# The last row tile of a matmul with layer norm: three quarters normalised from PSUM by VectorE, one quarter by GpSimd, stores on two queues

## The chip, the cores and the metric

The kernel runs on one core of a Trainium2 chip. The metric is the device time of one execution in microseconds, a median over runs. All times in this text are microseconds unless marked ns. One execution was recorded by the hardware profiler; its instruction times count from the start of its span, which runs from the first to the last recorded instruction. Differences of up to about 0.2% (0.5 us) can't be told from no change in this kernel.

## The reference

The inputs are `a` and `b`, both 2048 x 2048 in fp32, two vectors `gamma` and `beta` of length 2048, and a scalar `eps`.

```
x = np.matmul(a, b)
mean = np.mean(x, axis=-1, keepdims=True)
var = np.var(x, axis=-1, keepdims=True)
normalized = (x - mean) / np.sqrt(var + eps)
return (gamma * normalized + beta).astype(np.float32)
```

Each row of the product needs its mean and variance over all 2048 columns before any element of that row can be written out.

## The kernel before

The 2048 rows are cut into 16 row tiles of 128 rows (one row per partition), and each row tile into four quarters of 512 columns, numbered q = 0 to 3. A quarter is one PSUM bank: 128 x 512 fp32, written by 16 matmuls over the 16 blocks of the inner dimension (`mm`, line 99, fp16 operands). `b` stays in SBUF as fp16. Row tiles of `a` are transposed by TensorE or by DMA ahead of their use.

The first four row tiles are computed together while `a` and `b` arrive. From row tile 4 on the main loop (line 304) takes one row tile after the other, quarter by quarter. After a quarter's 16 matmuls, `evacuate` (lines 104 to 110) has ScalarE copy the bank into the SBUF tile `x` (line 109), and VectorE then reads that copy for the quarter's statistics (`bn_stats`, line 110). When the fourth quarter is in, `stats` (line 114) merges the four sets of statistics into mean and variance (`bn_aggr`, line 116), adds `eps` (line 118), and ScalarE takes the square root (line 120). VectorE's `reciprocal` (`inv`, line 141) gives `rstd`.

The normalisation of a quarter is two VectorE instructions in place on the SBUF tile, each a `scalar_tensor_tensor` over 128 x 512 fp32: `centre` (line 125), (x - mean) * gamma, and `scale` (line 131), x * rstd + beta. `store` (line 137) then issues a DMA to the output from the SP queue.

The schedule is written by hand: every engine executes its instructions in the order of the program. For all row tiles but the last, the normalisation is queued as two pieces in `backlog` and issued between the evacuations of the next row tile, so that VectorE does it while TensorE computes. For the last row tile (i = 15, lines 323 to 335) there is no next one. Nothing but its own normalisation and its four stores of 256 KB follows the last matmul: centre 0 and 1, rstd, scale and store 0, scale and store 1, centre 2 and 3, scale and store 2, scale and store 3. At the very end every engine waits until the SP engine has seen all DMA semaphores (line 366, the launch).

DMA semaphores go round: eight are used in turn by the DMAs that SP issues. The last four stores have the seventh, the eighth, the first and the second of them.

Of the kernel before, what the change touches and what calls it, by code (L numbers as in the profile page):

```python
# [9 lines left out]
FP32 = mybir.dt.float32  # L10
FP16 = mybir.dt.float16
AluOp = mybir.AluOpType
# [4 lines left out]
def kernel(  # L17
# [9 lines left out]
    nc = tc.nc  # L27
    P = 128
    M, K = a.shape
    K2, N = b.shape  # L30
# [3 lines left out]
    NB = 512  # L34
    n_nb = N // NB
# [18 lines left out]
    xpool = ctx.enter_context(tc.tile_pool(name="xpool", bufs=7))  # L54
    stat = ctx.enter_context(tc.tile_pool(name="stat", bufs=6))
# [8 lines left out]
    gamma_b = konst.tile([P, N], FP32)  # L64
    beta_b = konst.tile([P, N], FP32)
# [4 lines left out]
    xs = [None] * n_mt  # L70
    bnst = [None] * n_mt
    acc = {}
# [16 lines left out]
    def transpose_blocks(i, k0, n):  # L89

        t_ps = psum.tile([P, n, P], FP16, tag="ps", name=f"tps{i}_{k0}")
        for j in range(n):
            nc.tensor.transpose(t_ps[:, j, :], a16[i][:, ts(k0 + j, P)], ident)  # L93
        nc.scalar.copy(at[i][:, ds(k0, n), :], t_ps)  # L94

    def mm(i, q, kt):
        if (i, q) not in acc:
            acc[i, q] = bank(f"acc{i}_{q}")
        nc.tensor.matmul(  # L99
            acc[i, q], at[i][:, kt, :], b16[:, kt, ds(q * NB, NB)],  # L100
            start=(kt == 0), stop=(kt == n_kt - 1),
        )

    def evacuate(i, q):
        if xs[i] is None:
            xs[i] = xpool.tile([P, N], FP32, tag="x", name=f"x{i}")
            bnst[i] = stat.tile([P, n_nb, 6], FP32, tag="bnst", name=f"bnst{i}")
        qs = ds(q * NB, NB)
        nc.scalar.copy(xs[i][:, qs], acc[i, q])  # L109
        nc.vector.bn_stats(bnst[i][:, q, :], xs[i][:, qs])  # L110

    backlog = []

    def stats(i):
        mv = stat.tile([P, 2], FP32, tag="mv", name=f"mv{i}")
        nc.vector.bn_aggr(mv, bnst[i])  # L116
        ve = stat.tile([P, 1], FP32, tag="ve", name=f"ve{i}")
        nc.vector.tensor_tensor(ve, mv[:, 1:2], eps_t, AluOp.add)  # L118
        sq = stat.tile([P, 1], FP32, tag="sq", name=f"sq{i}")
        nc.scalar.activation(sq, ve, ActFn.Sqrt)  # L120
        return mv, sq

    def centre(i, q, mv):
        qs = ds(q * NB, NB)
        nc.vector.scalar_tensor_tensor(  # L125
            xs[i][:, qs], xs[i][:, qs], mv[:, 0:1], gamma_b[:, qs],
            AluOp.subtract, AluOp.mult)

    def scale(i, q, rstd):
        qs = ds(q * NB, NB)  # L130
        nc.vector.scalar_tensor_tensor(  # L131
            xs[i][:, qs], xs[i][:, qs], rstd, beta_b[:, qs],
            AluOp.mult, AluOp.add)

    def store(i, q0, nq):
        s = ds(q0 * NB, nq * NB)
        nc.sync.dma_start(out[ts(i, P), s], xs[i][:, s])

    def inv(i, sq):
        rstd = stat.tile([P, 1], FP32, tag="rstd", name=f"rstd{i}")  # L140
        nc.vector.reciprocal(rstd, sq)  # L141
        return rstd

    def queue_norm(i, mv, sq):

        got = {}

        def piece(q0):
            def run():
                centre(i, q0, mv)  # L150
                centre(i, q0 + 1, mv)
                if q0 == 0:
                    got["rstd"] = inv(i, sq)
                scale(i, q0, got["rstd"])
                scale(i, q0 + 1, got["rstd"])
                store(i, q0, 2)
            return run

        backlog.extend(piece(q) for q in range(0, n_nb, 2))

    def drain(n):
        for _ in range(min(n, len(backlog))):
            backlog.pop(0)()


    nc.vector.memset(zeros, 0.0)  # L166
    nc.vector.memset(ident, 0.0)
    nc.gpsimd.affine_select(
        out=ident, in_=ident, compare_op=AluOp.not_equal, fill=1.0,
# [92 lines left out]
    for what in order:  # L262
        if what[0] == "a":
            _, i, c = what
# [19 lines left out]
    for q in (2, 3):  # L284
# [3 lines left out]
        for p in range(n_open):  # L288
# [3 lines left out]
            if q == 3:  # L292
                mv, sq = stats(p)
# [10 lines left out]
    for i in range(n_open, n_mt):  # L304
        last = i == n_mt - 1
        if i + 1 < n_pe:
            at[i + 1] = atp.tile([P, n_kt, P], FP16, tag="at", name=f"at{i + 1}")
        if n_pe <= i + 3 < n_mt:
            at[i + 3] = atp.tile([P, n_kt, P], FP16, tag="at", name=f"at{i + 3}")
            nc.sync.dma_start_transpose(at[i + 3][:, :, :], a16[i + 3])  # L310
        for q in range(n_nb):
            for kt in range(n_kt):
                mm(i, q, kt)
                if i + 1 < n_pe and kt == 8 and q in (1, 2):
                    transpose_blocks(i + 1, (q - 1) * (n_kt // 2), n_kt // 2)
            evacuate(i, q)
            if q < n_nb - 1:
                drain(1)
        mv, sq = stats(i)
        if not last:  # L320
            queue_norm(i, mv, sq)
            drain(1)
        else:
            drain(len(backlog))
            for q in (0, 1):
                centre(i, q, mv)
            rstd = inv(i, sq)
            for q in (0, 1):
                scale(i, q, rstd)
                store(i, q, 1)  # L330
            for q in (2, 3):
                centre(i, q, mv)
            for q in (2, 3):
                scale(i, q, rstd)
                store(i, q, 1)


# [1 line left out]
_INS = ['a', 'b', 'gamma', 'beta', 'eps']  # L339
_OUTS = [((2048, 2048), 'float32')]  # L340
# [30 lines left out]
```

## Time and profile before

| what | us |
|---|---|
| median of 3 runs | 255.78 (255.48 to 255.9) |
| the profiled execution, its device time | 255.81 |
| its span | 254.0 |
| device time beyond the span | 1.8 |
| PE busy | 238.3 (94%) |
| DVE busy | 154.0 (61%) |
| ACT busy | 60.2 (24%) |
| POOL busy | 26.0 (10%) |

PE is TensorE, DVE is VectorE, ACT is ScalarE, POOL is GpSimd and SP is the engine that issues most DMAs; a name with a q behind it (SPq) is that engine's instruction queue. A group line gives line of the code, engine, operation, output and input tile with shapes and count, then busy time and the mean duration of one, then idle time of the engine before them and what ended it. A timeline line gives start, duration, engine, line and operation. A row may merge several instructions (x2).

TensorE is busy almost throughout, and its granted clock was 0.986 of full speed over the span. The last matmuls end at about 242.8, and 11 us of the span follow.

### The profile page before, as it was taken

How to read it: one execution, taken by the hardware profiler on the slowest of the kernel's cores; microseconds unless marked ns; L12 is line 12 of the kernel's file. 1: busy time of each engine (PE TensorE's matmuls, PEld its weight loads, DVE VectorE, ACT ScalarE, POOL GpSimd, SP SyncE). 2: the span in 40 equal slices, each digit the busy share in tenths (PEclk: the TensorE clock that was granted, in tenths of full speed). 3: DMA queues.
4: the chain of work that ended last, by engine and by line, in shares of the span. 5: the costliest groups of instructions: out<-in, count | busy, mean ns of one | idle time of the engine just before them, and what ended most of it. 6: DMA issues, size and time to landing. Idle time of an engine off the chain costs nothing.

```text
span 254.0 us, 3029 instructions
## 1 busy us (share of the span) xinstructions
PE 238.3 (94%) x1182; PEld 110.4 (43%) x1182; DVE 154.0 (61%) x275; ACT 60.2 (24%) x106; POOL 26.0 (10%) x52
## 2 busy tenths in 40 slices
PE   8899989999989999999999999999999999999920
PEld 3345444444444444454444444444444444444400
DVE  1555556203037999998959284765648291938563
ACT  2133216112074225232112121212121121112110
POOL 0000047767100001001000000000000000000000
PEclk9999999999999999999999999999999999999995
DMA  5999969999999759998996617090806222220304
GB/s 171 385 399 400 400 240 137 181 153 181 335 253 215 167 206 235 203 270 232 228 319 167 157 50 197 1 247 3 225 23 157 93 83 83 83 85 33 132 2 163
DMA packets 32782, 46.33 MB, mean 182 GB/s; under 512 B 18432, under 2 KB 22528, under 8 KB 32512
## 3 DMA queue, kind: packets, MB, share of 16 engines
q1 hardware_dynamic: 26144, 33.56, 39.9%
q0 software_dynamic: 6624, 12.59, 27.3%
q8 instruction: 9, 0.15, 0.2%
q14 instruction: 5, 0.04, 0.0%
HBM read 35.65 MB, written 16.78 MB: 206 GB/s over the span
## 4 chain that ended last, share of the span: by engine, by line
PE 80%; DMA 12%; DVE 3%; ACT 2%; SPq 0%; issue 0%; DVEq 0%
PE acc L99 79%; DMA b_st<-in_b_dram 7%; DMA a_st<-in_a_dram 5%; PE tps L93 1%; DVE x L125 1%; ACT at L94 1%; DVE x L131 1%; ACT x L109 1%; DVE bnst L110 1%; ACT L120 1%; DVE b L204 0%; DVEq L366 0%; DVE mv L116 0%; SPq L188 0%; ACT sq L120 0%
## 5 line engine op out<-in xcount | busy, mean ns | idle before, releaser
L99 PE MATMUL acc<-b,at 128*128 128x512 f16 x1024 | 225.3, 379 | 3.2 <-DVE b L204 1.5
L99 PEld LDWEIGHTS <-at 128*128 128x128 f16 x1024 | 99.2, 98 | 121.1 <-issue 3.3
L110 DVE BATCH_NORM_STATS2 bnst<-x 128x6 f32<-128x512 f32 x64 | 44.2, 691 | 74.0 <-ACT x L109 73.9
L109 ACT COPY x<-acc 128x512 f32<-128x512 f32 x64 | 37.5, 586 | 130.7 <-PE acc L99 130.5
L131 DVE SCALAR_TENSOR_TENSOR x<-x,rstd,beta_b 128x512 f32<-128x512 f32 x64 | 45.1, 746 | 0.6
L125 DVE SCALAR_TENSOR_TENSOR x<-x,mv,gamma_b 128x512 f32<-128x512 f32 x64 | 44.9, 743 | 0.0
L94 ACT COPY at<-tps 128x512 f16<-128x512 f16 (+1 forms) x24 | 17.4, 727 | 33.2 <-PE tps L93 33.2
L204 DVE CAST b<-b_st 128x1024 f16<-128x1024 f32 x16 | 11.1, 694 | 14.2 <-DMA b_st<-in_b_dram 14.2
L83 POOL DMA_DIRECT2D b<-in_b_dram x32 | 17.5, 551 | 6.4 <-DMA b<-in_b_dram 4.3
L303 POOL DMA_DIRECT2D a<-in_a_dram x11 | 5.8, 531 | 64.1 <-DMA at<-a 44.0
L93 PEld LDWEIGHTS <-a 128*128 128x128 f16 x128 | 9.2, 98 | 6.0 <-issue 0.6
L93 PE MATMUL tps<-ident,a 128*128 128x128 f16 x128 | 11.1, 219 | 0.1
L231 PE MATMUL warm<-zeros 128*128 128x512 f16 x30 | 9.2, 441 | 1.2 <-DVE zeros L166 1.2
L201 DVE CAST a<-a_st 128x512 f16<-128x512 f32 x16 | 6.8, 427 | 5.3 <-DMA a_st<-in_a_dram 5.3
L120 ACT ACTIVATE sq<-ve 128x1 f32<-128x1 f32 x16 | 3.2, 203 | 20.1 <-DVE ve L118 20.1
L231 PEld LDWEIGHTS <-zeros 128*128 128x128 f16 x30 | 3.1, 111 | 4.7 <-issue 2.1
L116 DVE BATCH_NORM_AGGREGATE mv<-bnst 128x2 f32<-128x24 f32 x16 | 4.2, 264 | 0.6
L212 POOL COPY gate<-b_st 128x1 f32<-128x1 f32 x1 | 0.7, 707 | 33.6 <-DMA b_st<-in_b_dram 33.6
L118 DVE TENSOR_TENSOR ve<-mv,eps_t 128x1 f32<-128x1 f32 x16 | 2.5, 159 | 0.5
L141 DVE RECIPROCAL rstd<-sq 128x1 f32<-128x1 f32 x16 | 2.5, 156 | 0.0
L94 ACT ACT_TABLE_LOAD x1 | 1.3, 1283 | 0.7 <-PEq L352 0.7
L120 ACT ACT_TABLE_LOAD x1 | 1.3, 1283 | 0.0
(11 smaller groups left out, 2.7 us busy)
## 6 DMA issues: line engine op xcount, KB each, us to landing
out_dram<-x SPq DMA_DIRECT2D x30, 512.0 KB, 3.5
b_st<-in_b_dram SPq DMA_DIRECT2D x16, 512.0 KB, 7.8
a<-in_a_dram POOLq DMA_DIRECT2D x12, 512.0 KB, 9.1
a_st<-in_a_dram SPq DMA_DIRECT2D x16, 256.0 KB, 7.2
b<-in_b_dram POOLq DMA_DIRECT2D x32, 128.0 KB, 5.7
gamma_b<-in_gamma_dram POOLq DMA_DIRECT2D x1, 1024.0 KB, 9.9
beta_b<-in_beta_dram POOLq DMA_DIRECT2D x1, 1024.0 KB, 12.8
out_dram<-x SPq DMA_DIRECT2D x4, 256.0 KB, 2.6
```

Source lines behind the costliest of these rows:

```text
L83: nc.gpsimd.dma_start(b16[:, kt, ds(c0, w)], b[ts(kt, P), ds(c0, w)])
L93: nc.tensor.transpose(t_ps[:, j, :], a16[i][:, ts(k0 + j, P)], ident)
L94: nc.scalar.copy(at[i][:, ds(k0, n), :], t_ps)
L99: nc.tensor.matmul(acc[i, q], at[i][:, kt, :], b16[:, kt, ds(q * NB, NB)], start=(kt == 0), stop=(kt == n_kt - 1),)
L109: nc.scalar.copy(xs[i][:, qs], acc[i, q])
L110: nc.vector.bn_stats(bnst[i][:, q, :], xs[i][:, qs])
L120: nc.scalar.activation(sq, ve, ActFn.Sqrt)
L125: nc.vector.scalar_tensor_tensor(xs[i][:, qs], xs[i][:, qs], mv[:, 0:1], gamma_b[:, qs], AluOp.subtract, AluOp.mult)
L131: nc.vector.scalar_tensor_tensor(xs[i][:, qs], xs[i][:, qs], rstd, beta_b[:, qs], AluOp.mult, AluOp.add)
L201: nc.vector.tensor_copy(a16[i][:, ts(c, KW)], a_st[c][:, ts(i, KW)])
L204: nc.vector.tensor_copy(b16[:, k, 0:NH], b_st[k // 2][:, ts(k % 2, NH)])
L231: nc.tensor.matmul(warm, zeros[:, 0:P], zeros, start=True, stop=True)
```

## The change

For row tile 15 `evacuate` is replaced by `evacuate_last`: only quarter 1 is still copied to SBUF by ScalarE; the statistics of all four quarters are read by VectorE straight from the PSUM banks. The tail is replaced by `finish`: quarters 0, 2 and 3 are normalised by VectorE, the first step in place in PSUM (`first`) and the second from PSUM into the SBUF tile (`second`); quarter 3's second step is cut into two halves of 256 columns, each with a store of its own. Quarter 1 is normalised by GpSimd in three instructions from the SBUF copy. Quarters 2 and 1 are stored from the SP queue, quarter 0 and the halves of quarter 3 from the ACT queue. VectorE's new order is first 2, first 3, rstd, first 0, second 2, second 0, second 3a, second 3b. Nothing before row tile 15 changes.

```diff
+    PQ = 1
+    def evacuate_last(i, q):
+        if xs[i] is None:
+            xs[i] = xpool.tile([P, N], FP32, tag="x", name=f"x{i}")
+            bnst[i] = stat.tile([P, n_nb, 6], FP32, tag="bnst", name=f"bnst{i}")
+        if q == PQ:
+            nc.scalar.copy(xs[i][:, ds(q * NB, NB)], acc[i, q])
+        nc.vector.bn_stats(bnst[i][:, q, :], acc[i, q])
+
+    def finish(i, mv, sq):
+        x = xs[i]
+        def first(q):
+            nc.vector.scalar_tensor_tensor(
+                acc[i, q], acc[i, q], mv[:, 0:1], gamma_b[:, ds(q * NB, NB)],
+                AluOp.subtract, AluOp.mult)
+        def second(q, c0, w, eng):
+            s = ds(q * NB + c0, w)
+            nc.vector.scalar_tensor_tensor(
+                x[:, s], acc[i, q][:, ds(c0, w)], rstd, beta_b[:, s],
+                AluOp.mult, AluOp.add)
+            eng.dma_start(out[ts(i, P), s], x[:, s])
+        first(2)
+        first(3)
+        rstd = inv(i, sq)
+        s = ds(PQ * NB, NB)
+        nc.gpsimd.tensor_scalar(
+            x[:, s], x[:, s], mv[:, 0:1], rstd, AluOp.subtract, AluOp.mult)
+        nc.gpsimd.tensor_tensor(x[:, s], x[:, s], gamma_b[:, s], AluOp.mult)
+        nc.gpsimd.tensor_tensor(x[:, s], x[:, s], beta_b[:, s], AluOp.add)
+        first(0)
+        second(2, 0, NB, nc.sync)
+        second(0, 0, NB, nc.scalar)
+        nc.sync.dma_start(out[ts(i, P), s], x[:, s])
+        second(3, 0, NB // 2, nc.scalar)
+        second(3, NB // 2, NB // 2, nc.scalar)
@@ main loop
+            if last:
+                evacuate_last(i, q)
+                drain(len(backlog) if q > 0 else 1)
+                continue
             evacuate(i, q)
@@ after the quarters of a row tile
         else:
-            drain(len(backlog))
-            for q in (0, 1):
-                centre(i, q, mv)
-            rstd = inv(i, sq)
-            for q in (0, 1):
-                scale(i, q, rstd)
-                store(i, q, 1)
-            for q in (2, 3):
-                centre(i, q, mv)
-            for q in (2, 3):
-                scale(i, q, rstd)
-                store(i, q, 1)
+            finish(i, mv, sq)
```

## The prediction

> **What bounds the kernel now.** I read the chain of waits first. Over the whole span it is TensorE (80%) and DMA; the change touches only what follows the last matmul, so I read the chain again for the last 20 us, then the timeline, the DMA view and the busy time by window there.
>
> ```profile
> 235.85 6.92 PE acc L99 x32
> ...
> 242.80 0.59 ACT x L109
> ...
> 243.42 0.70 DVE bnst L110
> ...
> 244.14 0.28 DVE mv L116
> ...
> 244.44 0.04 DVE ve L118
> ...
> 244.52 1.41 DVE x L125 x2
> 245.94 0.09 DVE rstd L141
> ...
> 246.04 1.41 DVE x L131 x2
> 247.46 1.32 DVE x L125 x2
> 248.78 0.66 DVE x L131
> 249.44 0.66 DVEq L366
> ```
>
> Columns: start, duration, piece. From 242.80 on there is one serial chain: ScalarE's copy of quarter 3, its statistics, then VectorE instruction after instruction without a gap. The last piece, put down to line 366, is the last `scale` (the timeline has `scale` x2 from 248.70 for 1.41, so VectorE ends at 250.11). The chain view stops there; the stores go on. The next lines are from the timeline, the DMA view from 236 to 256 (GB/s in slices of half a microsecond, then the last row's stores), and the windows (length, busy time of PE, weight loads, DVE, ACT and POOL, clock, DMA share, GB/s):
>
> ```profile
> 246.82 3.64 SPq L137 DMA_DIRECT2D out_dram<-x  x4
> ```
> ```profile
> GB/s 0 0 0 229 410 401 8 0 0 0 0 0 0 0 0 0 0 0 0 0 0 0 0 262 369 340 78 0 152 377 344 176 0 0 0 0 0 0 0 0
> ...
> out_dram<-x SPq DMA_DIRECT2D x4, 256.0 KB, 2.6
> ```
> ```profile
> 246.00:250.10 4.10, 0.00 (x0) 0.00 (x0) 4.07 (x7) 0.00 (x0) 0.00 (x0) 0.58 0.37 128
> 250.10:252.80 2.70, 0.00 (x0) 0.00 (x0) 0.01 (x1) 0.00 (x0) 0.00 (x0) 0.50 0.56 194
> 252.80:254.05 1.25, 0.00 (x0) 0.00 (x0) 0.00 (x0) 0.00 (x0) 0.00 (x0) 0.50 0.00 0
> ```
>
> VectorE is full (4.07 of 4.10) until 250.1; the last store, issued at 250.13, lands 2.65 later, at 252.78; then 1.25 of semaphore waits close the kernel. The tail is thus 7.3 of chain, 2.65 of last store, 1.25 of closing. Only the first two can move.
>
> **What the change does, part by part.** Clock times are this execution's; 242.80 is when quarter 3's matmuls are done for a reader.
>
> *The copy goes.* The last bn_stats starts where the copy started, 242.80 in place of 243.42: 0.62 saved. The copies of quarters 0 and 2 go too; ScalarE idles 2.87 before each such copy, so they are worth nothing. Quarter 1's statistics wait for ScalarE's copy as before, about 3 us ahead of need: nothing.
>
> *PSUM as a VectorE operand.* The trace has no VectorE row on PSUM. On SBUF a 128x512 `scalar_tensor_tensor` (STT) lasts 0.745 and the next starts 0.66 after it. VectorE's CAST takes 0.427 for 512 columns and 0.694 for 1024, a fixed part of 0.16; ScalarE's copies from PSUM, 0.586 and 1.008, have a fixed part of 0.16 as well. So PSUM may cost nothing (or save a few hundredths), or double the fixed part, 0.16; I take half, 0.08 per instruction. One more bound: if reading and writing one bank in place halves the rate, each `first` costs some 0.5 more.
>
> *VectorE's chain.* Statistics to aggregation took 0.72, now 0.80: aggregation at 243.60. From there to the first STT 0.38, as before: `first` 2 at 243.98. Two steps of 0.74: reciprocal at 245.46 (before 245.85; the square root is done by 244.4 and stays hidden). Then `first` 0; `scale` followed the reciprocal by 0.19 with a wait on it, `first` 0 has no such wait: 0.10, at 245.56. `second` 2 runs from 246.30 to 247.12, `second` 0 from 247.04 to 247.87, 3a from 247.78. Half the columns take off 0.25: 3b from 248.27 to 248.85. That is 1.26 earlier than 250.11: 0.62 for the copy, 1.32 for two STTs given to GpSimd, 0.09 at the reciprocal, less 0.16 for cutting quarter 3, less eight PSUM surcharges (0.64); the rest is rounding.
>
> *GpSimd's three instructions.* They start when rstd is done, 245.46 + 0.15, plus a hop, 245.69. The trace has little elementwise work on GpSimd:
>
> ```profile
> L212 POOL COPY gate<-b_st 128x1 f32<-128x1 f32 x1 | 0.7, 707 | 33.6 <-DMA b_st<-in_b_dram 33.6
> ...
> L168 POOL TENSOR_SCALAR_AFFINE_SELECT ident<-ident 128x128 f16<-128x128 f16 x1 | 0.3, 289 | 0.8 <-DVE ident L167 0.8
> ...
> L352 POOL MEMSET const-float32-0.0<- 128x1 f32 x1 | 0.1, 99 | 0.2 <-issue 0.2
> ```
>
> The select takes 0.289 for 128 columns, a one-element memset 0.099: 0.19 per 128 columns, so 0.86 for 512 with one input (1.16 if all of the row scales). With two inputs: between 0.86 and twice that, 1.72. I take 1.2, a little under the middle, since the select evaluates a pattern beside each element. So 0.86 + 1.2 + 1.2 and two hops of 0.05, 3.36 (bounds 2.7 and 4.7): GpSimd ends at 249.05, after VectorE. It becomes the last engine.
>
> The Trainium skill (GPSIMD Engine Reference, 3.1) speaks against the move: elementwise work belongs on VectorE, and an add of two 2048-column fp32 inputs took 4497 ns on GpSimd, 2293 on VectorE. Scaled to 512 columns that is an estimate of 1.12 each, with which the sum would be 0.16 lower. The rule speaks of one engine's price; here the quarter runs beside 3.2 us of VectorE work.
>
> *Stores.* x2 is issued on SP at 247.15, x0 on ACT at 247.90, 3a and 3b on ACT at 248.38 and 248.88, x1 on SP at 249.08. An SP issue holds the queue 0.33; ACT has 0.48 between its own. Behind x1's wait for GpSimd stand only SP's closing waits; 3a and 3b are on the other queue and pass it. ACT issues no DMA in the trace: its first may cost nothing extra, or what SP's first did (256 KB landed 3.7 after issue against 2.6, so 1.1). That falls on x0, which has it to spare; I take nothing. 3b (128 KB) lands by 248.88 + 2.6 = 251.5 at worst. A 512 KB store lands 2.6 after its issue too (line 137 at 236.92), and at the 400 GB/s of the slices 1.3 of that is transfer; 256 KB alone would land after 1.95, with a neighbour in flight after 2.65. x1 follows the end of 3b: the middle, 2.3, landing 251.38 in place of 252.78.
>
> *Closing.* SP checks the DMA semaphores in turn, some 0.06 a step; x1 has the first of the round where the last store before had the second: one step more, 0.06. The 1.8 outside the span: unchanged.
>
> Sum: 252.78 - 251.38 - 0.06 = 1.34. The profiled execution took 255.81, 0.03 above the median of the runs; 255.81 - 1.34 = **254.5**.
>
> **Rivals.**
>
> *GpSimd at its upper price: no change.* With 4.7 in place of 3.36, x1 is issued at 250.42 and lands at 252.72: 255.8. Banks at half rate in place do nearly the same from the other side: the reciprocal moves by 1.0, x1 to 250.1, the time to 255.5. For it: the only large GpSimd row is 128 columns wide, in fp16. Against: each two-input instruction must be as slow as two selects. It is this case from a GpSimd sum of 4.2 up.
>
> *VectorE and GpSimd block each other: slower.* The gate COPY above handles one element and took 0.707. It ran from 35.20 to 35.91, a VectorE CAST from 35.17 to 35.86: GpSimd stood until VectorE let go. If the PSUM instructions with gamma or beta do the same, the two alternate: `first` 0 to 246.4, GpSimd to 247.25, `second` 2 to 248.1, GpSimd to 249.3, `second` 0 to 250.1, GpSimd to 251.3, 3b to 252.35, issued then, landing 2.0 later (128 KB) at 254.35, 1.57 late: 257.4. It decides once x1 or 3b is issued later than about 250.5. Against it: the CAST has both its sides in SBUF, while each STT beside GpSimd has a single SBUF tensor to read.
>
> The Trainium skill (SBUF — State Buffer, Who interferes with whom) draws its line there: a VectorE instruction competes with GpSimd if it has two SBUF inputs or runs in a two-port mode; one with at most one SBUF input, outside those modes, does not. By it the sum stands as it is, by the gate's row alone it would be the rival's. No row of this trace shows the one-input case.
>
> *GpSimd cheap and PSUM free.* With 2.7 and no surcharge GpSimd ends at 248.15 and 3b at 248.2; x1 lands by 250.1 to 250.8: 253.2 to 253.9.
>
> **How the numbers follow.** Faster by over 0.2% (0.5 us, about what a measurement of this kernel can tell from no change): 0.74, of which 0.10 is the cheap case. Within 0.2%, GpSimd or PSUM at the dear end: 0.11. Slower, by blocking or by both dear ends together: 0.15. The faster cases span 253.2 to 255.3. The range, 253.4 to 256.0, takes in the no-change case and leaves out most of the blocking (0.13) and a little at the bottom (0.04).
>
> **What would show it.** The last bn_stats starts at 242.8 and lasts 0.77; PSUM STTs start 0.74 apart; the reciprocal stands at 245.5; GpSimd's rows read 0.86, 1.2 and 1.2 from 245.7 on without gaps; VectorE has no gap until 248.85; x1 is the last issue, near 249.1; the DMA is silent by 251.4, with 1.3 of closing. Wrong would be GpSimd instructions that end where VectorE's end, or VectorE gaps the length of a GpSimd instruction (blocking); GpSimd past 250.4; VectorE steps near 1.2. If ACT's stores took over 2.6 to land, 3b and not x1 would end the kernel.

## The result, and the profile after

The changed kernel is slower: 256.6 us median of 8 runs (255.98 to 256.79) against 255.69 for the kernel before, ratio 1.0037 with a 95% interval of 1.0028 to 1.0047. The forecast was 254.5, with a range of 253.4 to 256.0. The profiled execution took 256.59 with a span of 254.8, against 255.81 and 254.0.

VectorE did better than forecast; GpSimd and the closing of the kernel did worse. The timeline of the changed kernel from the last statistics on (start, duration, engine, line, operation):

```profile
242.72 0.70 DVE L175 BATCH_NORM_STATS2 bnst<-acc 128x6 f32<-128x512 f32 x1 [2.75 <-PE acc L99]
...
243.83 1.41 DVE L181 SCALAR_TENSOR_TENSOR acc<-acc,mv,gamma_b 128x512 f32<-128x512 f32 x2
...
245.15 0.15 DVE L141 RECIPROCAL rstd<-sq 128x1 f32<-128x1 f32 x1
...
245.41 2.07 POOL L196 TENSOR_SCALAR x<-x,mv,rstd 128x512 f32<-128x512 f32 x1 [114.35 <-DVE rstd L141]
245.87 2.18 DVE L187 SCALAR_TENSOR_TENSOR x<-acc,rstd,beta_b 128x512 f32<-128x512 f32 x4
246.64 0.33 SPq L190 DMA_DIRECT2D out_dram<-x  x1
247.30 1.38 ACTq L190 DMA_DIRECT2D out_dram<-x  x3
247.57 1.26 POOL L198 TENSOR_TENSOR x<-x,gamma_b 128x512 f32<-128x512 f32 x1
248.91 1.26 POOL L199 TENSOR_TENSOR x<-x,beta_b 128x512 f32<-128x512 f32 x1
250.20 0.33 SPq L203 DMA_DIRECT2D out_dram<-x  x1
```

VectorE ends at 245.87 + 2.18 = 248.05, 2.06 before the 250.11 of the kernel before. GpSimd's first instruction takes 2.07, its three instructions together 4.76, and it ends at 250.17. Quarter 1's store, issued at 250.20, is the last, 0.07 later than the last store before.

The windows of the same stretch (length, busy PE, weight loads, DVE, ACT, POOL, clock, DMA share, GB/s) and the closing instructions of the launch line, two of its DRAINs among them (count, ns min/median/max, first and last start). A DRAIN is one of the closing instructions of an engine's queue; it can start while the engine's last computation still runs, as GpSimd's does here at 248.9:

```profile
245.40:248.10 2.70, 0.00 (x0) 0.00 (x0) 2.65 (x5) 0.00 (x0) 2.60 (x2) 0.91 0.24 89
248.10:250.20 2.10, 0.00 (x0) 0.00 (x0) 0.00 (x0) 0.00 (x0) 1.99 (x2) 0.50 0.88 260
250.20:252.60 2.40, 0.00 (x0) 0.00 (x0) 0.00 (x0) 0.00 (x0) 0.00 (x0) 0.50 0.30 110
252.60:254.80 2.20, 0.00 (x0) 0.00 (x0) 0.00 (x0) 0.00 (x0) 0.00 (x0) 0.50 0.00 0
```
```profile
L399 POOLq DRAIN  x3: 46/93/5137, 248.9 to 254.5; - x3
L399 SPq DRAIN  x3: 7/7/7, 253.1 to 254.3; - x3
```

The first window has VectorE and GpSimd both full: they work side by side. In the second, 2.1 us, GpSimd works alone. The last store lands at 252.6, 0.14 earlier than before, and yet the closing after it takes 2.2 in place of 1.25. The two DRAIN lines above say why: SP has seen all its semaphores and drains at 253.1, as before, but GpSimd's first closing DRAIN starts at 248.9 and takes 5.137, so it ends at 254.0; the other engines leave only then. GpSimd's last instruction had ended at 250.17, 3.84 earlier. In the profile before, GpSimd's DRAIN stands far ahead of the end:

```profile
L366 POOLq DRAIN  x3: 51/93/7283, 131.0 to 253.8; - x3
L366 SPq DRAIN  x3: 7/7/7, 253.2 to 253.5; - x3
```

It started at 131.0, behind GpSimd's last load, took 7.283 and was over by 138.3. The 0.8 between SP's closing (253.2) and the end of GpSimd's DRAIN (254.0) is the loss.

### The profile page after: what moved, and what is told of

Its sections match the earlier page's. It is cut to its first block, busy times and chain, and to the rows that moved or that the text cites. A ratio compares the mean times of both kernels' runs of the same rounds, so it can differ in the third digit from the quotient of the medians.

```text
span 254.8 us, 3033 instructions
## 1 busy us (share of the span) xinstructions
PE 238.8 (94%) x1182; PEld 110.5 (43%) x1182; DVE 152.8 (60%) x274; ACT 58.4 (23%) x103; POOL 30.5 (12%) x55
## 4 chain that ended last, share of the span: by engine, by line
PE 80%; DMA 12%; ACT 2%; DVE 2%; POOL 1%; POOLq 1%; issue 0%; SPq 0%
PE acc L99 79%; DMA b_st<-in_b_dram 7%; DMA a_st<-in_a_dram 5%; PE tps L93 1%; ACT at L94 1%; POOL x L196 1%; POOLq L399 1%; ACT L120 1%; POOL x L198 0%; DVE acc L181 0%; ACT x L109 0%; DVE bnst L175 0%; DVE bnst L110 0%; DVE b L246 0%; DVE mv L116 0%
## 5 line engine op out<-in xcount | busy, mean ns | idle before, releaser
L110 DVE BATCH_NORM_STATS2 bnst<-x 128x6 f32<-128x512 f32 x60 | 41.5, 691 | 68.8 <-ACT x L109 68.7
L109 ACT COPY x<-acc 128x512 f32<-128x512 f32 x60 | 35.1, 585 | 120.7 <-PE acc L99 120.6
L131 DVE SCALAR_TENSOR_TENSOR x<-x,rstd,beta_b 128x512 f32<-128x512 f32 x60 | 42.3, 747 | 0.5
L125 DVE SCALAR_TENSOR_TENSOR x<-x,mv,gamma_b 128x512 f32<-128x512 f32 x60 | 42.1, 743 | 0.0
L196 POOL TENSOR_SCALAR x<-x,mv,rstd 128x512 f32<-128x512 f32 x1 | 2.1, 2072 | 114.3 <-DVE rstd L141 114.3
L175 DVE BATCH_NORM_STATS2 bnst<-acc 128x6 f32<-128x512 f32 x4 | 2.8, 695 | 4.6 <-PE acc L99 4.6
## 6 DMA issues: line engine op xcount, KB each, us to landing
a_st<-in_a_dram SPq DMA_DIRECT2D x16, 256.0 KB, 7.3
out_dram<-x SPq DMA_DIRECT2D x2, 256.0 KB, 2.5
```

What stands on the lines that cost most here:

```text
L125: nc.vector.scalar_tensor_tensor(xs[i][:, qs], xs[i][:, qs], mv[:, 0:1], gamma_b[:, qs], AluOp.subtract, AluOp.mult)
L131: nc.vector.scalar_tensor_tensor(xs[i][:, qs], xs[i][:, qs], rstd, beta_b[:, qs], AluOp.mult, AluOp.add)
```

## Experiments

Theory A: the time is set by GpSimd, by the price of its first instruction and by a DRAIN that ends a fixed 3.84 after its last one. Rival B: the ACT queue or the PSUM operands cost the time, and GpSimd is only beside it. Rival C: it is the late store of quarter 1.

One reading helps with all that follows. In every recorded execution TensorE takes 169.12 from the first matmul of row tile 4 to the start of the last one; that first matmul starts between 72.94 and 73.41, so executions differ ahead of it. So a change to the tail is read most closely from the start of the first instruction that reads the last quarter to the end of the span; this stretch is called the tail below. It is 242.80 to 254.05 before, which is 11.25, and 242.72 to 254.79 in the changed kernel, 12.07.

**GpSimd taken out (e1_no_pool).** The changed kernel with quarter 1 on VectorE like the others.

```diff
-        if q == PQ:
-            nc.scalar.copy(xs[i][:, ds(q * NB, NB)], acc[i, q])
...
-        s = ds(PQ * NB, NB)
-        nc.gpsimd.tensor_scalar(
-            x[:, s], x[:, s], mv[:, 0:1], rstd, AluOp.subtract, AluOp.mult)
-        nc.gpsimd.tensor_tensor(x[:, s], x[:, s], gamma_b[:, s], AluOp.mult)
-        nc.gpsimd.tensor_tensor(x[:, s], x[:, s], beta_b[:, s], AluOp.add)
         first(0)
         second(2, 0, NB, nc.sync)
         second(0, 0, NB, nc.scalar)
-        nc.sync.dma_start(out[ts(i, P), s], x[:, s])
+        first(1)
+        second(1, 0, NB, nc.sync)
```

> Quarter 1 goes back to VectorE (from PSUM, in place, like the other three); GpSimd has no work in the last row tile; two store queues stay. Theory A (GpSimd's long chain and its late DRAIN are what cost the time): VectorE steps of 0.66 as in the changed kernel, VectorE ends near 249.4, the last half store is issued on ACT near 249.4 and lands near 251.8, GpSimd's DRAIN ends early, the time is 254.6 to 255.0, ratio 0.995 to 0.997. Rival B (the second store queue or the PSUM operands cost the time, GpSimd hides): the time stays at 256.2 to 256.8.

255.19 against 255.65 on the same chip, ratio 0.9981 (0.9969 to 0.9993): faster than the kernel before, though by less than the 0.995 to 0.997 that A expected. The tail takes 10.70, 0.55 less than before: VectorE's work ends at 249.30, 6.78 after it first reads the last quarter, where the kernel before needs 7.31 from the start of the copy. B falls: the PSUM operands and the ACT queue are still there.

**One queue (e2_no_pool_one_queue).** The kernel of e1 with all five stores issued from SP.

```diff
-        second(0, 0, NB, nc.scalar)
+        second(0, 0, NB, nc.sync)
...
-        second(3, 0, NB // 2, nc.scalar)
-        second(3, NB // 2, NB // 2, nc.scalar)
+        second(3, 0, NB // 2, nc.sync)
+        second(3, NB // 2, NB // 2, nc.sync)
```

> As e1_no_pool, with all five stores issued from SP. Theory A: SP needs 0.38 per issue and VectorE gives a store every 0.66 (0.39 for the last two halves), so the same time as e1_no_pool within 0.2, 254.6 to 255.1. Rival B (the ACT queue is dear): 0.3 or more below e1_no_pool. Third view (the ACT queue saves issue time): 0.2 to 0.4 above e1_no_pool.

255.03, ratio 0.9976 (0.9963 to 0.9990), and a tail of 10.69. The intervals of e1 and e2 overlap almost wholly: without GpSimd's wait on SP the second queue neither costs nor brings anything that can be measured.

**A single-column copy at the end (e4_tiny_end).** The kernel before, plus one GpSimd instruction that nobody waits for:

```diff
                 scale(i, q, rstd)
                 store(i, q, 1)
+            probe = konst.tile([P, 1], FP32)
+            nc.gpsimd.tensor_copy(probe, xs[i][:, ds(N - 1, 1)])
```

> The kernel before, with one added GpSimd copy of a single column that waits for the last scale; no store waits for it. Theory A1 (a GpSimd compute instruction makes the closing DRAIN end a fixed 3.8 after it): copy at 250.15 to 250.3, DRAIN until about 254.1, the span about 254.85, the time 256.6, ratio 1.003. Rival A2 (the DRAIN's length goes with the size of the work in GpSimd, or it is the stores that it waits for): DRAIN ends by 253.3, the time stays at 255.7.

256.69, ratio 1.0040 (1.0027 to 1.0052): the loss of the whole change, from a copy of 0.18 us. From the timeline and the launch line:

```profile
250.31 0.18 POOL L337 COPY probe<-x 128x1 f32<-128x1 f32 x1 [117.90 <-DVE x L131]
```
```profile
L368 POOLq DRAIN  x3: 51/93/4042, 250.3 to 254.8; - x3
```

The copy ends at 250.49, the DRAIN at 250.3 + 4.04, 254.3: 3.84 after the copy, as in the changed kernel, where the last instruction took 1.26. The size of the work does not matter, and no store was late here.

**The same copy earlier (e7_early_probe).** It waits for rstd in place of the last `scale`.

```diff
             rstd = inv(i, sq)
+            probe = konst.tile([P, 1], FP32)
+            nc.gpsimd.tensor_copy(probe, rstd)
```

> The kernel before with one added one-column GpSimd copy, as in e4_tiny_end, but waiting for the last rstd (near 246.0) in place of the last scale. Theory A (a fixed 3.84 after the last GpSimd compute instruction): DRAIN ends near 250.1, hidden under the stores, the time within 0.2 of the kernel before. Rival (any late GpSimd compute costs the closing 0.9): 256.6.

255.75 against 255.73, ratio 1.0004 (0.9990 to 1.0018), no difference.

```profile
L368 POOLq DRAIN  x3: 46/93/4047, 245.8 to 253.5; - x3
```

The copy starts at 245.78, the DRAIN (4047 ns from 245.8) ends at 249.8, below the stores. A late GpSimd instruction costs nothing as such; it costs when it ends less than 3.84 before SP's closing.

**A memset in its place (e13_memset_end).** As e4, with an instruction that reads nothing, behind a one-column VectorE copy that orders it.

```diff
+            nc.vector.tensor_copy(probe, xs[i][:, ds(N - 1, 1)])
+            nc.gpsimd.memset(probe, 0.0)
```

> e4_tiny_end with a GpSimd memset, which reads nothing, in place of the copy, behind one added one-column VectorE copy. If every GpSimd compute instruction is followed by 3.84 of DRAIN: the DRAIN ends near 254.3 and the time is 256.6 to 256.8. If only an instruction that reads has it: as the kernel before, 255.7 to 255.9, as at the start of the trace, where a DRAIN behind four memsets was over 0.05 after the last.

256.84, ratio 1.0036 (1.0025 to 1.0046). The memset ends at 250.43, the DRAIN (3956 ns) at 254.27, again 3.84 later. So it is not the reading. At the start of the span a DRAIN follows four memsets and takes 0.18 in all; what the closing one waits for was not found.

**Quarter 1's store freed (e8_store_free).** The changed kernel, but GpSimd works on a second copy of quarter 1 that nobody stores. Quarter 1 itself is stored as it comes from the matmul: its normalisation is left out of the output.

```diff
+        y = konst.tile([P, NB], FP32)
+        nc.scalar.copy(y, acc[i, PQ])
         nc.gpsimd.tensor_scalar(
-            x[:, s], x[:, s], mv[:, 0:1], rstd, AluOp.subtract, AluOp.mult)
+            y, y, mv[:, 0:1], rstd, AluOp.subtract, AluOp.mult)
...
```

> The changed kernel, GpSimd's three instructions on a second copy of quarter 1 that nobody stores; quarter 1 of the last row tile is stored as it comes from the matmul (that part of the computation is left out), so its store waits for nothing. Theory A (the DRAIN decides, the late store is hidden under it): stores are down by 251.5, GpSimd's rows and its DRAIN stand as in the changed kernel, the time stays within 0.2 of 256.6. Rival (the late store decides): 255.0 to 255.4.

256.73, ratio 1.0045 (1.0029 to 1.0061).

```profile
L401 POOLq DRAIN  x3: 46/93/5142, 249.0 to 254.7; - x3
L401 SPq DRAIN  x3: 7/7/7, 252.2 to 254.4; - x3
```

SP drains at 252.2, 0.9 earlier than in the changed kernel; GpSimd's DRAIN (5142 ns from 249.0) still ends near 254.2, and the time does not move. C falls: the late store is hidden under the DRAIN.

**GpSimd's first instruction replaced (e3_act_step).** In the changed kernel ScalarE does (x - mean) * rstd from PSUM; GpSimd keeps the other two.

```diff
-        if q == PQ:
-            nc.scalar.copy(xs[i][:, ds(q * NB, NB)], acc[i, q])
...
-        nc.gpsimd.tensor_scalar(
-            x[:, s], x[:, s], mv[:, 0:1], rstd, AluOp.subtract, AluOp.mult)
+        nmr = stat.tile([P, 1], FP32, tag="ve", name=f"nmr{i}")
+        nc.vector.scalar_tensor_tensor(
+            nmr, mv[:, 0:1], -1.0, rstd, AluOp.mult, AluOp.mult)
+        nc.scalar.activation(x[:, s], acc[i, PQ], ActFn.Identity, bias=nmr, scale=rstd)
```

> The changed kernel, with GpSimd's 2.07 us tensor_scalar replaced by one ScalarE instruction from PSUM (x * rstd - mean * rstd, the factor from one added one-column VectorE instruction); GpSimd keeps the two two-input instructions. Theory A (GpSimd's last instruction plus 3.84 sets the end): GpSimd ends at 248.9 to 249.1 in place of 250.17, its DRAIN at 252.8 to 253.0, the time 255.3 to 255.6, about 1.2 below the changed kernel. Rival B (the second queue or PSUM): no change from 256.6.

255.41, ratio 0.9990 (0.9978 to 1.0002), as A expected: 1.2 below the changed kernel, each set against the kernel before on its own chip.

```profile
246.14 1.26 POOL L198 TENSOR_TENSOR x<-x,gamma_b 128x512 f32<-128x512 f32 x1 [115.49 <-ACT x L197]
247.48 1.26 POOL L199 TENSOR_TENSOR x<-x,beta_b 128x512 f32<-128x512 f32 x1
```
```profile
L399 POOLq DRAIN  x3: 51/102/5136, 247.4 to 253.1; - x3
L399 SPq DRAIN  x3: 7/7/13, 252.1 to 252.8; - x3
```

GpSimd ends at 248.74, 1.43 earlier; 0.25 of that is this execution's earlier tail (last statistics at 242.48 in place of 242.72), so 1.2 comes from the edit. The DRAIN ends at 252.6, 3.84 after it, and is still the last by 0.4. The end moves with GpSimd's last instruction.

**The price of GpSimd's instructions (e5_prices).** Eight of them on a scratch tile, behind everything else, VectorE idle.

```diff
+            probe = konst.tile([P, NB], FP32)
+            g.tensor_copy(probe, xs[i][:, s])
+            g.tensor_tensor(probe, probe, gamma_b[:, s], AluOp.mult)
+            g.tensor_scalar(probe, probe, mv[:, 0:1], rstd, AluOp.subtract, AluOp.mult)
+            g.tensor_scalar(probe, probe, 0.5, 2.0, AluOp.subtract, AluOp.mult)
+            g.tensor_scalar(probe, probe, mv[:, 0:1], None, AluOp.subtract)
+            g.tensor_scalar(probe, probe, 0.5, None, AluOp.subtract)
...
```

> The kernel before, with eight GpSimd instructions on a scratch tile behind the last scale, VectorE idle, no store waiting: copy, two-input multiply, two-operation tensor_scalar with two per-partition operands, the same with two constants, one operation with a per-partition operand, one operation with a constant (all 128x512), then the two-input multiply and the two-operand tensor_scalar with 256 columns. Theory A (2.07 is the instruction's own price): 2.05 for the two-operand form alone, 1.26 for the two-input multiply; halves at about 0.65 and 1.05; DRAIN ends 3.8 after the last of them. Rival (2.07 holds a wait for VectorE's port): 0.8 to 1.3 for the two-operand form with VectorE idle.

```profile
249.87 0.61 POOL L339 COPY probe<-x 128x512 f32<-128x512 f32 x1 [119.32 <-DVE x L131]
250.57 1.26 POOL L340 TENSOR_TENSOR probe<-probe,gamma_b 128x512 f32<-128x512 f32 x1
251.94 2.08 POOL L341 TENSOR_SCALAR probe<-probe,mv,rstd 128x512 f32<-128x512 f32 x1
254.11 1.92 POOL L342 TENSOR_SCALAR probe<-probe 128x512 f32<-128x512 f32 x1
256.13 1.56 POOL L343 TENSOR_SCALAR probe<-probe,mv 128x512 f32<-128x512 f32 x1
257.79 1.49 POOL L344 TENSOR_SCALAR probe<-probe 128x512 f32<-128x512 f32 x1
259.36 0.72 POOL L346 TENSOR_TENSOR probe<-probe,gamma_b 128x256 f32<-128x256 f32 x1
260.19 1.23 POOL L347 TENSOR_SCALAR probe<-probe,mv,rstd 128x256 f32<-128x256 f32 x1
```

The two-operation form costs 2.08 with VectorE idle, 2.07 beside VectorE's PSUM instructions: the price is the instruction's own, and no wait for VectorE is in it. Every `tensor_scalar` with one tensor input costs more than `tensor_tensor` with two. The second operation adds 0.4 to 0.5, the per-partition operands 0.07 to 0.16. The kernel took 267.8 (a single execution): the eight rows run from 249.87 to 261.42, and the DRAIN ends 3.84 after the last of them here too.

**GpSimd beside VectorE on SBUF (e6_pool_beside_sbuf).** The kernel before with GpSimd's share of the change alone: the statistics and VectorE's steps stay on SBUF, each with two SBUF inputs.

```diff
             drain(len(backlog))
+            centre(i, 2, mv)
+            centre(i, 3, mv)
+            rstd = inv(i, sq)
+            nc.gpsimd.tensor_scalar(
+                x[:, s], x[:, s], mv[:, 0:1], rstd, AluOp.subtract, AluOp.mult)
+            nc.gpsimd.tensor_tensor(x[:, s], x[:, s], gamma_b[:, s], AluOp.mult)
+            nc.gpsimd.tensor_tensor(x[:, s], x[:, s], beta_b[:, s], AluOp.add)
+            centre(i, 0, mv)
+            scale(i, 2, rstd)
+            store(i, 2, 1)
...
```

> The kernel before with GpSimd's share of the change alone: copies, statistics and six VectorE steps from SBUF as before, quarter 1 on GpSimd, all stores on SP, quarter 1's last. If two SBUF inputs make VectorE and GpSimd exclude each other, GpSimd's two-input instructions take 1.9 in place of 1.26 or VectorE shows gaps of 0.5 to 2; if not, GpSimd has 2.07, 1.26, 1.26 from 246.1 and VectorE steps of 0.66 without a gap. Time 257.3 without blocking, 258 to 259 with.

258.75 (a single execution). On SBUF the two do get in each other's way:

```profile
246.02 3.65 POOL L330 TENSOR_SCALAR x<-x,mv,rstd 128x512 f32<-128x512 f32 x1 [115.36 <-DVE rstd L141]
249.76 1.26 POOL L332 TENSOR_TENSOR x<-x,gamma_b 128x512 f32<-128x512 f32 x1
251.10 1.26 POOL L333 TENSOR_TENSOR x<-x,beta_b 128x512 f32<-128x512 f32 x1
```
```profile
246.48 2.42 DVE L131 SCALAR_TENSOR_TENSOR x<-x,rstd,beta_b 128x512 f32<-128x512 f32 x3
```

GpSimd's first instruction takes 3.65 in place of 2.08 while VectorE runs; three VectorE steps take 2.42 in place of 2.07, the first two at 0.74 each and the third at 1.10. The two later ones, with VectorE idle, keep their 1.26. The stretch fell on the one-input instruction and not, as the expectation had it, on the two-input ones, which came too late to meet VectorE.

**A better tail (e10_whole_last, e11_last_in_round, e12_merge_alone).** e10 is e2 with quarter 3's second step and store in one piece:

```diff
-        second(3, 0, NB // 2, nc.sync)
-        second(3, NB // 2, NB // 2, nc.sync)
+        second(3, 0, NB, nc.sync)
```

> e2_no_pool_one_queue with quarter 3's second step and store in one piece (512 columns). The halves cost VectorE 0.13 and SP one more issue, and let the last transfer be 128 KB in place of 256 KB: if the last transfer's size decides, 0.1 to 0.4 slower than e2_no_pool_one_queue; if the instruction counts, 0.1 faster. The ratio to the kernel before 0.997 to 0.999.

255.21, ratio 0.9977 (0.9964 to 0.9990), as e2: the halves bring and cost nothing that can be measured.

e11 is e2 with the stores of row tiles 11 to 13 merged, so that the last store of the kernel has the last semaphore that SP checks; e12 is the same edit on the kernel before, its tail untouched; its last store has the last but one.

```diff
+        whole = i in (11, 12, 13)
...
-                store(i, q0, 2)
+                if not whole:
+                    store(i, q0, 2)
+                elif q0 > 0:
+                    store(i, 0, 4)
```

> e2_no_pool_one_queue with the two stores of row tiles 11, 12 and 13 merged into one each (1 MB), so that the last store of the kernel has the last semaphore of SP's closing round and no checks stand behind it. Five checks of 0.06 fall off the end: 0.3 below e2_no_pool_one_queue, 254.7 to 254.9, ratio to the kernel before 0.996 to 0.997. If the checks run beside something else at the end, no change.

> The kernel before, its tail untouched, with the stores of row tiles 11, 12 and 13 merged as in e11_last_in_round. The last store then has the seventh semaphore of the round in place of the second, and five checks of 0.06 fall off the end. If the closing checks are all there is to the merge: 0.3 faster than the kernel before, ratio 0.9985 to 0.9992. If merging the stores also helps the row tiles in front: 0.6 to 0.9 faster, ratio 0.9965 to 0.9978.

e11 took 254.34 against 255.84, ratio 0.9943 (0.9931 to 0.9956); e12 254.9 against 255.86, ratio 0.9966 (0.9952 to 0.9979). Both beat what the closing semaphore waits alone explain. In e12's trace 0.19 passes from the last store's semaphore to SP's second DRAIN, where it was 0.49 before, and its tail is 10.96 in place of 11.25: 0.3, and no more. In e11 the tail is 10.36 against 10.69 in e2, again 0.3. TensorE's 169.12 is the same with and without the merge, so the recorded executions hold no further gain from it. The medians, of five runs each, are lower by some 0.6 more in both (the recorded executions, 254.87 and 255.24, lie above them); where that comes from was not recorded and stays open. e11 is faster than both kernels.

## Why the prediction was wrong, step by step

*The copy goes.* Right. The last bn_stats starts at 242.72 and lasts 0.70.

*PSUM as a VectorE operand.* The surcharge of 0.08 was wrong: it is nothing. bn_stats takes 0.698 from PSUM and 0.694 from SBUF, and two STTs 1.41 on either, in place in one bank too. The Trainium skill (Perfetto Trace Analysis, Optimizing Scalar/DVE Operations) gives VectorE a higher access overhead on PSUM than on SBUF, about 125 ns against 60; the rows here show no such difference, and they decide. VectorE's end at 248.05, 0.80 ahead of the 248.85 forecast, is 0.64 from these eight surcharges and the rest mostly an execution whose tail starts 0.08 earlier.

*GpSimd's three instructions.* This step failed first. The `tensor_scalar` was put at 0.86, with 1.16 as the upper bound, by scaling the affine select of 128 columns; it measured 2.07. The select is no near relative: another operation, on fp16. The two `tensor_tensor` were right, 1.26 each for 1.2. The sum was 4.76 for 3.36, just past its upper bound of 4.7; as GpSimd started at 245.41 in place of 245.69, its end moved by 1.12. By this term alone x1 lands 0.14 before the last store did, and the first rival, no change, would have been the case.

*Closing.* This step failed too, and turned no change into a loss. It was priced at 1.25 plus one check of 0.06, from the profile before, in which GpSimd was long idle and its DRAIN over at 138.3. With GpSimd at work to the end the DRAIN became the last event: 3.84 after GpSimd's last instruction. Had GpSimd ended at 249.05 as forecast, the DRAIN would have ended at 252.9, and with the 0.78 of span and 1.8 beyond the span that follow it the time would have been near 255.5, not 254.5; e3, where GpSimd ended as far behind the last matmul as that, took 255.41. So neither miss alone makes the kernel slower; a late GpSimd and a DRAIN behind it together do.

The two together: x1's landing at 252.64 in place of 251.38 is 1.26, of which GpSimd's end is 1.12; the DRAIN behind SP's closing is 0.8; 254.5 + 2.06 is 256.56.

*VectorE and GpSimd block each other.* The time fell on the slower side, which had been given 0.15, but not by this rival's mechanism: GpSimd's first instruction took 2.07 beside VectorE, 2.08 alone. The effect itself exists, in e6, where each VectorE instruction reads two SBUF tensors. This is the line that the Trainium skill (SBUF — State Buffer, Who interferes with whom) draws, two SBUF inputs against one, and both cases, this kernel and e6, agree with it. The gate copy's 0.71, on which the rival rested, was not the price of one column: that form took 0.18 in e4, with VectorE idle, and 0.18 in e7, beside a VectorE step on SBUF.

*Stores.* Issue times followed the engines as said. ACT's issues hold its queue 0.38 to 0.41 in place of SP's 0.33, the three stores on ACT land 2.8 to 3.1 after issue, more than the 2.6 that the prediction named as a limit, but the last of them lands at 251.09 and none ends the kernel. x1 landed 2.4 after its issue (forecast 2.3).

## What to carry to other kernels

Work given to an idle engine is priced by that very instruction form on that engine; another operation's row, scaled, was wrong by more than its bounds. An engine that was idle at the end of a program has its closing hidden there: before giving it late work, ask when its own DRAIN can end. Here VectorE alone from PSUM, without GpSimd, was the gain that the change held (0.9976 to 0.9981), and the loss was all GpSimd's.

## What the runs showed that was not expected

- GpSimd's closing DRAIN ended 3.84 us after its last compute instruction in all eight kernels that had one in the tail (3.837 to 3.844), behind a memset of 0.10 as behind a `tensor_scalar` of 1.23.
- On GpSimd a 128x512 fp32 `tensor_scalar` costs 1.49 to 2.08, more than a `tensor_tensor` with two tensor inputs, 1.26, and a copy 0.61.
- VectorE read and wrote PSUM at SBUF's price: 0.698 against 0.694 for bn_stats, 1.41 for two STTs on either.
- Merging three pairs of 512 KB stores into 1 MB stores, well ahead of the end, went with a median 0.9 us lower (0.9966, five runs); its trace shows 0.3 of that, at the closing, by the order of SP's semaphores.
